# First layer's output product: two of four weight chunks by seven products of sums

## The chip, the cores and the metric

The kernel runs on one core of one Trainium2 chip. The metric is device time of one execution in microseconds (us). The engines named below are PE (matrix products; PEld is its weight load), DVE (elementwise work), ACT (activations, copies, casts), POOL (elementwise work and the issue of some DMAs) and SP (the issue of the other DMAs). Each runs its own instruction queue in order; semaphores join them.

## The reference

Two layers of a block with sparse attention, multi-scale pooling and a gated sum, on 16 meta tokens and 512 tokens (T = 528) with D = 1024. What bears on this change is the last line of a layer, and the norm that begins the next:

```python
def rms_norm(x, g):
    xf = x.astype(jnp.float32)
    y = xf * lax.rsqrt(jnp.mean(xf * xf, axis=-1, keepdims=True) + EPS)
    return (y * g.astype(jnp.float32)).astype(x.dtype)
...
    g_a, g_b = jnp.split(jax.nn.sigmoid(merge), 2, axis=-1)
    return x + jnp.einsum('btd,de->bte', g_a * y_a + g_b * y_b, w_out)
```

The output product multiplies the merged branches M (528 tokens by 1024) with `w_out` (1024 by 1024) and adds it to the residual. All values are float32.

## The kernel before, in words

**Precision by parts.** PE multiplies in a reduced form (fp32r). Each operand is therefore kept as a high part (a cast) and a low part (value minus high part), and a product is three matmuls: high by high, high by low, low by high. The merged branches lie transposed, 8 blocks k of 128 features by 528 tokens, in `hhi` and `hlo`. The high parts are cast by ACT (L1479), the low parts are subtracted by POOL, and for the last block by DVE.

**Weights** come in chunks of 256 output columns (for `w_out`), each loaded by SP as two `raw` tiles from a ring of four, and split into `w` tiles from a ring of eight. A tile's place is free for the next load or split when its last reader is done. There are three ways to split a chunk. In the plain one ACT casts (L206) and DVE subtracts (two `w<-raw,w` of 128x1024). For the chunks in `by_dma` ACT writes the negated cast (L220), a DMA issued by POOL adds the raw values onto it in place (L221), and ACT casts again (L225); DVE does nothing. For the chunks in `mixed`, `mixed_prep` (L257) forms sums of the four blocks of the weight matrix: one by a DMA that adds in place before the rest (`first_sum`, L255), the others by DVE and one more DMA (L284). ACT casts seven operands (L269), and DVE subtracts seven low parts of 128x512.

**Two forms of product.** `dense` (L596) multiplies one block of 128 output columns with one half of the tokens: 8 k blocks by 3 = 24 matmuls into one of three PSUM banks `d`. `group_of_products` (L1044) takes a chunk of 256 columns by two halves of the tokens as a 2x2 block product done with seven products instead of eight (Strassen's scheme as Winograd ordered it): 7 products of 4 k blocks by 3 = 84 matmuls. Its operands on the token side are the four quarters of the left matrix and sums of them. The first layer's gates use it already, with 264 tokens a half (`mix_gates`), and so does the second layer's output product for its last two chunks (`sums_of_merged` and `mix_out`, 256 tokens a half). `product` (L1054) calls weight preparation until the operand that it needs has been issued.

**The first layer's end.** After the gates, two chunks of branch A are multiplied (L1468): for each of 8 blocks j and each half, 12 matmuls, then on DVE `ta` = (`ta` + 1) times the product, plus `zb` (both in `ta`), the cast to `hhi` on ACT and the low part `hlo` on POOL. Then POOL makes the tables of the next layer (`tables`, L481: `gk`, `Cg`, `Sg`). The output product follows: chunks 0 and 1 in `dense` form for both token halves (272 and 256), then chunks 2 and 3 together, the first half of the tokens for all four column blocks, then the second half. After each group DVE adds it to the residual (`res`), ACT squares it (`tq`), POOL adds up the squares (`sqs`). After the first half's last group `stats` (L1517) sums the squares over the features on PE, POOL takes the power, and `norm_half` (L511) turns the result on PE, multiplies on DVE (8 blocks `nf`), casts on ACT and subtracts low parts on DVE and POOL, with the low part of a block three blocks behind its product. This runs beside the second half's products. The next layer starts with `plain_trio` (L579), products of `nf` in plain float32, and goes on with `tok_group`, which needs `hhi` and `hlo`.

**Order.** PE and DVE run in the order in which the code records them: `later(fn, n)` puts work n groups on, `group_done` runs what is due and one item of weight preparation. ACT, POOL and SP are ordered by a scheduler. All recorded calls of PE and DVE carry the line of a helper, L63, so they are told apart by their tiles.

Of the kernel before, what the change touches and what calls it, by code (L numbers as in the profile page):

```python
# [11 lines left out]
OP = mybir.AluOpType  # L12
# [79 lines left out]
def tile_block(ctx: ExitStack, tc: tile.TileContext, x, meta, w_in, pool_w, w_a, w_b, w_out, rows, hgain, c_tab, out):  # L92
# [10 lines left out]
    def f(ap):  # L103
        return ap.bitcast(F32)
# [406 lines left out]
    def norm_half(l, hf, rstd, lag=1, pool=(1, 3, 5, 7), warm_up=False):  # L511
# [11 lines left out]
        nf = [NF[0][k // 4][:, k % 4, a:a + n] for k in range(KT)]  # L523
        for k in range(KT + lag):
            if k < KT:
                t = nf[k]
                dve.scalar_tensor_tensor(t, RES[0][:, k, a:a + n], parT[:, l * 8 + k:l * 8 + k + 1], rb[:, :n],
                                         op0=OP.mult, op1=OP.mult)
                end = act.copy(hhi[:, k, a:a + n], t)
            if k >= lag:  # L530
                j = k - lag
                (gp if j in pool else dve).tensor_sub(hlo[:, j, a:a + n], nf[j], f(hhi[:, j, a:a + n]))
        return end.ins
# [61 lines left out]

    def dense(w, mt_, a, n, rhs=H, kt=KT, late=False):  # L596
        ps = bank("d")
# [5 lines left out]
        for e, (ww, r, k) in enumerate(steps):  # L603
            pe.matmul(ps[:, :n], ww[k][:, c], r[:, k, a:a + n], start=e == 0, stop=e == len(steps) - 1)
            if (e + 1) % (len(steps) // parts) == 0 and e + 1 < len(steps):
                (group_done if (e + 1) * 4 // len(steps) == 2 and parts == 4 else half_done)()
        return ps

# [527 lines left out]

    def sums_of_merged(ta):

        c0, c1 = slice(16, 272), slice(272, 528)
        t1 = one.tile([128, 2, 4, 256], F32R, tag="D", name="osum1")  # L1140
        t4 = []
        t2 = [tmp.tile([128, 4, 128], F32R, tag="P", name="osum2", bufs=PB).rearrange("p (s a) c -> p s (a c)", s=2)
              for _ in range(4)]
        t3 = [tmp.tile([128, 544], F32R, tag="L", name="osum3", bufs=LB)[:, :512].rearrange("p (s c) -> p s c", s=2)
              for _ in range(4)]

# [5 lines left out]

        def sums(k):
            a0, a1, b1 = ta[k][:, c0], ta[k][:, c1], ta[4 + k][:, c1]
# [13 lines left out]
        def last_high(k):  # L1168
            if not t4:
                t4.append(one.tile([128, 2, 4, 256], F32R, tag="C", name="osum4"))  # L1170
            act.copy(t4[0][:, 0, k], ta[4 + k][:, c0])
# [25 lines left out]

    def mix_out(operands):
        base = popped[0] - progress[W["use"]]
        for q in range(2):  # L1200
            def add(eh, t, src):
                j = 4 + 2 * q + eh
                d = RES[0][:, j, 16 + 256 * t:272 + 256 * t]
                dve.scalar_tensor_tensor(d, src, -0.5 if eh else 0.5, d, op0=OP.mult, op1=OP.add)
                later(lambda: turned_out(j, t), 2)

            def total(eh, t, ps, part):
                o = sheet(256, "c")[:, :256]
                dve.tensor_tensor(o, ps[:, :256], part, op=OP.add)
                add(eh, t, o)  # L1210

            group_of_products(q, base, 256, operands, total, add)

# [57 lines left out]
    for l in range(2):  # L1271
# [196 lines left out]
        for c in range(2):  # L1468
            w = chunk()
            if l and c:  # L1470
                first, sums, lows, fourth, last_high, last_low, operands = sums_of_merged(ta)
# [21 lines left out]
        if l == 0:  # L1493
# [4 lines left out]
            dve.memset(mm, 1.0)  # L1498
            def out_group(w, mi, j, halves):
                for hf, a, n, o in halves:  # L1500
                    ps = dense(w, mi, a, n, late="k" if j == hf == 0 else False)
                    d = RES[0][:, j, a:a + n]
                    dve.scalar_tensor_tensor(d, ps[:, :n], 0.5, d, op0=OP.mult, op1=OP.add)
                    if j == 0:
                        act.activation(sq[:, a:a + n], d, AF.Square, scale=D ** -0.5)
                    elif j < KT - 1:
                        t = tmp.tile([128, HB], F32, tag="tt", name="tq", bufs=6)
                        act.activation(t[:, :n], d, AF.Square, scale=D ** -0.5)
                        gp.tensor_tensor(sq[:, a:a + n], sq[:, a:a + n], t[:, :n], op=OP.add)
                    else:  # L1510
# [17 lines left out]

            for c in range(2):
                w = chunk()  # L1530
                for mi in range(2):
                    out_group(w, mi, 2 * c + mi, halves)
            w2 = chunk()
            flush_prep()
            w3 = chunk(ahead=False)
            for hs in (halves[:1], halves[1:]):
                for c, w in ((2, w2), (3, w3)):
                    for mi in range(2):
                        out_group(w, mi, 2 * c + mi, hs)
                    if c == 2 and hs[0][0] == 1:  # L1540
                        w_prep_enqueue()
                if hs[0][0] == 0:
                    later(lambda: stats(0), 1)
                    later(lambda: norm_half(1, 0, mm, LAG2), 2)
            hooks = {0: lambda: stats(1), 1: lambda hf: None if hf else norm_half(1, 1, mm, LAG3)}
        else:
# [34 lines left out]
            later(lambda: [last_low(k) for k in (2, 3)], 4)  # L1581
            mix_out(operands)
            rows(1, 4, w, flush)
# [52 lines left out]
```

## Time and profile before

| | |
|---|---|
| median of 3 runs (lowest to highest) | 734.21 us (733.96 to 734.82) |
| the profiled execution's own time | 735.03 us |
| its span in the trace | 733.2 us |
| mean granted PE clock | 1.00 |
| PE busy, share of the span | 723.7 us, 99% |
| DVE / ACT / POOL busy | 597.2 / 491.4 / 262.3 us |
| output product of the first layer | 328.4 to 377.2 us in the trace |

Rows of a timeline are: start, duration, engine, line, operation, output tile <- input tiles, shapes, how many were merged, and in brackets how long the engine sat idle before and what ended that. The profile models the end of a matmul, so a row's duration there overlaps with the next; rates of PE are taken from one start to another. The same holds for DVE, where one instruction's end overlaps with the start of the next.

### The profile page before, as it was taken

The page shows a single profiled execution, that of the slowest core. Times are in us where ns is not written, and L with a number is a line of the kernel's source. Part 1 is how long each engine was busy: PE and PEld are TensorE (multiplying, and loading weights), DVE is VectorE, ACT ScalarE, POOL GpSimd, SP SyncE. Part 2 cuts the span into 40 slices and gives each one's busy share as a digit, 9 for nine tenths or more (in the row PEclk, how much of TensorE's full clock was granted, in tenths as well). Part 3 has the DMA queues.
Part 4 walks back from the last instruction along what each step waited for, and adds up shares of the span by engine and source line. Part 5 has one row for each costly group of instructions (what it writes and reads, how often), then busy time and mean ns, then how long its engine had stood idle before and what let it go on. Part 6 is the DMA issues. An engine that isn't in the chain of part 4 may idle for free.

```text
span 733.2 us, 15958 instructions
## 1 busy us (share of the span) xinstructions
PE 723.7 (99%) x5853; PEld 697.0 (95%) x5853; DVE 597.2 (81%) x1488; ACT 491.4 (67%) x1125; POOL 262.3 (36%) x345
## 2 busy tenths in 40 slices
PE   9999999999999999999999999999999999999998
PEld 8999998899999999999999989998899899999997
DVE  6877999998998875894358779999989988768774
ACT  6779635676888886543246796367788888775643
POOL 3751174721223311173256411857042231116210
PEclk9999999999999999999999999999999999999999
DMA  8777755974655333633422788667564554438832
GB/s 268 234 180 166 168 138 116 238 149 91 148 113 136 81 92 97 211 124 130 132 89 87 180 185 200 155 162 163 112 160 105 134 116 91 113 108 269 201 90 71
DMA packets 103566, 106.41 MB, mean 145 GB/s; under 512 B 5008, under 2 KB 83632, under 8 KB 103488
## 3 DMA queue, kind: packets, MB, share of 16 engines
q1 hardware_dynamic: 91888, 74.89, 33.5%
q0 software_dynamic: 11520, 30.41, 23.4%
q8 instruction: 46, 0.75, 0.4%
q14 instruction: 32, 0.26, 0.1%
q10 hardware_dynamic: 80, 0.08, 0.0%
HBM read 66.41 MB, written 8.55 MB: 102 GB/s over the span
## 4 chain that ended last, share of the span: by engine, by line
PE 79%; DVE 12%; issue 4%; ACT 2%; DMA 2%; POOL 1%; DVEq 0%; POOLq 0%; ACTq 0%
PE d L63 65%; PE a L63 10%; PE v L63 4%; DVE w L63 3%; DVE t L63 1%; DVE lt L63 1%; DMA w<-raw 1%; DVE sc L63 1%; DVE m L63 1%; ACT lt L832 1%; DVE zb L63 1%; DVE nf L63 1%; DVE c L63 0%; DMA raw<-s 0%; DVE sila L63 0%
## 5 line engine op out<-in xcount | busy, mean ns | idle before, releaser
L63 PE MATMUL d<-hhi,w 128*128 128x256 f32 (+3 forms) x1392 | 279.2, 292 | 1.6 <-DVE c L63 1.6
L63 PEld LDWEIGHTS d<-hhi,w 128*128 128x128 f32 x1392 | 222.3, 188 | 5.2 <-DVE c L63 2.0
L63 PE MATMUL d<-hlo,w 128*128 128x256 f32 (+3 forms) x696 | 189.8, 289 | 0.0
L63 DVE TENSOR_TENSOR w<-raw,w 128x512 fp32r<-128x512 f32 (+1 forms) x156 | 121.8, 787 | 14.5 <-ACT w L269 14.3
L63 PEld LDWEIGHTS d<-hlo,w 128*128 128x128 f32 x696 | 131.3, 189 | 1.4 <-issue 0.2
L63 PE MATMUL d<-hsum,w 128*128 128x264 f32 (+1 forms) x720 | 95.1, 285 | 0.2
L63 PEld LDWEIGHTS d<-hsum,w 128*128 128x128 f32 x720 | 89.7, 188 | 1.2 <-issue 0.3
L63 PE MATMUL d<-w,hhi 128*128 128x256 f32 x576 | 86.1, 287 | 0.6 <-DVE w L63 0.6
L269 ACT CAST w<-raw 128x512 fp32r<-128x512 f32 x132 | 78.5, 623 | 3.0 <-DMA raw<-s 2.3
L63 PEld LDWEIGHTS d<-w,hhi 128*128 128x128 f32 x576 | 74.7, 188 | 5.3 <-issue 2.9
L255 POOL DMA_DIRECT2D raw<-raw x22 | 20.5, 931 | 109.3 <-DMA raw<-in_w_in_dram 16.3
L63 DVE MATCH_REPLACE8 sc<-m,sc 128x400 f32<-128x400 f32 (+2 forms) x100 | 54.4, 547 | 0.0
L63 DVE MAX8 m<-sc 128x8 f32<-128x400 f32 (+2 forms) x100 | 53.4, 557 | 0.9
L221 POOL DMA_DIRECT2D w<-raw x34 | 31.8, 966 | 60.9 <-ACT w L220 44.7
L832 ACT ACTIVATE lt<-lt,mn,NR 128x144 f32<-128x144 f32 (+3 forms) x64 | 42.2, 661 | 13.2 <-DVE mn L63 13.0
L63 PE MATMUL d<-mhi,w 128*128 128x272 f32 (+2 forms) x192 | 46.1, 326 | 1.0 <-ACT sq L681 0.9
L63 PE MATMUL d<-w,hlo 128*128 128x256 f32 x288 | 45.5, 281 | 0.0
L284 POOL DMA_DIRECT2D raw<-s x22 | 19.2, 871 | 65.5 <-DVE s L63 29.0
L847 POOL TENSOR_SCALAR pm<-lt,rs 128x16 f32<-128x16 f32 x48 | 28.0, 612 | 38.8 <-DVE rs L63 28.6
L753 ACT ACTIVATE r<-a,wab 128x272 f32<-128x272 f32 (+2 forms) x80 | 35.5, 487 | 8.7 <-PE a L63 8.2
L1481 POOL TENSOR_TENSOR hlo<-ta,hhi 128x256 fp32r<-128x256 f32 (+1 forms) x28 | 26.6, 961 | 40.9 <-PE d L63 28.7
L690 POOL TENSOR_TENSOR t<-t,t 128x256 f32<-128x256 f32 (+1 forms) x34 | 30.6, 900 | 24.6 <-DVE t L63 24.3
(259 smaller groups left out, 1566.2 us busy)
## 6 DMA issues: line engine op xcount, KB each, us to landing
raw<-in_w_in_dram SPq DMA_DIRECT2D x88, 256.0 KB, 3.3
w<-raw POOLq DMA_DIRECT2D x34, 512.0 KB, 5.8
raw<-in_w_in_dram SPq DMA_DIRECT2D x32, 512.0 KB, 4.3
raw<-in_w_out_dram SPq DMA_DIRECT2D x12, 512.0 KB, 3.6
raw<-raw POOLq DMA_DIRECT2D x22, 256.0 KB, 4.0
raw<-s POOLq DMA_DIRECT2D x22, 256.0 KB, 3.3
kept<-res SPq DMA_DIRECT2D x16, 264.0 KB, 2.8
res<-kept SPq DMA_DIRECT2D x16, 264.0 KB, 5.2
```

The source lines that it names most:

```text
L63: return fn(*a, **k)
L221: gp.dma_start(t, raws[c][s], accum_op=OP.add)
L255: gp.dma_start(raws[c][0][:, 1], raws[c][0][:, 0], accum_op=OP.add)
L269: act.copy(t[:, 0], blk[src[n]])
L284: gp.dma_start(blk["a12"], blk["s2"], accum_op=OP.add)
L690: added[0] = gp.tensor_tensor(t1[:m, :256], t1[:m, :256], t2[:m, :256], op=OP.add).ins
L753: act.activation(r[:, n - 1::-1] if i == 0 else r[:, o:o + e], ps[:, :e], AF.Relu, scale=wab[:, i, h:h + 1])
L832: act.activation(L[hh][:, :n], L[hh][:, :n], AF.Exp, scale=NR[:, i, h:h + 1], bias=mn[:, hh:hh + 1], accum_out=sm[:, hh:hh + 1])
L847: (gp if j < 3 else dve).tensor_scalar(pms[i][:, 2 * j + hh, :], L[hh][:, 0:16], rs[:, hh:hh + 1], None, op0=OP.mult)
L1481: pool_end = gp.tensor_sub(hlo[:, j, a:a + n], d, f(hhi[:, j, a:a + n]))
```

## The change

Only the first layer's output product and what feeds it are touched.

- Chunk 0 of `w_out` is split `by_dma`; chunks 1 and 2 become `mixed`. These are the second and third of four.
- The token sums that the groups need (`sums_of_merged`, now with the halves' start and width as arguments) are formed from `ta`: first differences (`first`) while branch A's second chunk runs, the other sums, high parts and low parts in four steps beside chunk 0, one after each `dense`.
- Chunks 1 and 2 run as two `group_of_products` of 264 tokens a half.
- Chunk 3 alone runs by token halves (272, then 256). `stats` for the first half goes into the middle of the second half's first group, `norm_half` into the middle of its last. With the argument `KT + 1` `norm_half` issues all eight products and casts first, and the low parts after the group.

```diff
+        if l == 0:
+            by_dma.add(len(chunks) - 4)
+            mixed |= {len(chunks) - 3, len(chunks) - 2}
...
-        for k in range(KT + lag):
+        for k in range(KT + lag % (KT + 1)):
...
+        if lag > KT:
+            return lambda: [low(j) for j in range(KT)]
...
-    def sums_of_merged(ta):
+    def sums_of_merged(ta, s0, n2):
-        c0, c1 = slice(16, 272), slice(272, 528)
+        c0, c1 = slice(s0, s0 + n2), slice(s0 + n2, s0 + 2 * n2)
...
+                if l == 0 and c:
+                    if mi == 0:
+                        prep_one()
+                    first(mi)
...
-            for c in range(2):
-                w = chunk()
-                for mi in range(2):
-                    out_group(w, mi, 2 * c + mi, halves)
-            w2 = chunk()
-            flush_prep()
-            w3 = chunk(ahead=False)
-            for hs in (halves[:1], halves[1:]):
-                for c, w in ((2, w2), (3, w3)):
-                    for mi in range(2):
-                        out_group(w, mi, 2 * c + mi, hs)
...
-                if hs[0][0] == 0:
-                    later(lambda: stats(0), 1)
-                    later(lambda: norm_half(1, 0, mm, LAG2), 2)
+            w = chunk()
+            sums(0)
+            sums(1)
+            steps = deque([lambda: [sums(2), sums(3)], lambda: [lows(0), lows(1), fourth_all()],
+                           lambda: [lows(2), lows(3), last_high(0), last_high(1)],
+                           lambda: [last_high(2), last_high(3), last_low(0), last_low(1)]])
...
+            for mi in range(2):
+                out_group(w, mi, mi, halves, None, lambda: steps.popleft()())
+            last_low(2)
+            last_low(3)
+            mix_out(operands, 2, s0, n2, lambda j, t, d: squares(n2 * t, n2, d))
+            w = chunk(ahead=False)
+            for mi in range(2):
+                out_group(w, mi, 6 + mi, halves[:1])
+            w_prep_enqueue()
+            out_group(w, 0, 6, halves[1:], lambda: stats(0))
+            rest = []
+            out_group(w, 1, 7, halves[1:], lambda: rest.append(norm_half(1, 0, mm, KT + 1)), lambda: later(rest[0], 0))
```

What this does to DVE's queue is seen just behind branch A's last low part. In the rows, `osum` tiles hold the token sums' parts, `s` is a sum of weight blocks, `w` a low part of weights. Before, from that low part on (`msq` is a fill of the statistics):

```order
L63 TENSOR_TENSOR hlo<-ta,hhi 128x256
L63 MEMSET msq 128x5
L63 SCALAR_TENSOR_TENSOR res<-d,res 128x272
L63 SCALAR_TENSOR_TENSOR res<-d,res 128x256
L63 TENSOR_TENSOR w<-raw,w 128x1024
L63 SCALAR_TENSOR_TENSOR res<-d,res 128x272
```

Now, the last twelve rows up to the low part of weights that the first group's third product needs (the last row). Ahead of them, behind the same `hlo` row, stand nineteen more instructions of 128x264 and two `res` rows:

```order
L63 TENSOR_TENSOR w<-raw,w 128x512
L63 TENSOR_TENSOR s_5050<-raw 128x512
L63 TENSOR_TENSOR w<-raw,w 128x512
L63 SCALAR_TENSOR_TENSOR res<-d,res 128x272
L63 TENSOR_TENSOR osum_4961<-ta,osum_4961 128x264
L63 TENSOR_TENSOR osum_4964<-ta,osum_4964 128x264
L63 TENSOR_TENSOR osum_4961<-ta,osum_4961 128x264
L63 TENSOR_TENSOR osum_4965<-ta,osum_4965 128x264
L63 TENSOR_TENSOR raw<-s_5050,raw 128x512
L63 SCALAR_TENSOR_TENSOR res<-d,res 128x256
L63 TENSOR_TENSOR osum_4961<-ta,osum_4961 128x264 x4
L63 TENSOR_TENSOR w<-s_5050,w 128x512
```

Between branch A's end and the first group's third product DVE has 27 instructions of 128x264, five of 128x512 and four `res` additions, where it had the four `res` additions and two subtractions of 128x1024.

POOL's queue at the same place, which holds branch A's low parts, the tables and the squares. Before:

```order
L1481 TENSOR_TENSOR hlo<-ta,hhi 128x256
L484 TENSOR_SCALAR gk<-gains 128x64
L494 TENSOR_TENSOR Cg<-consts,gk 128x320
L495 TENSOR_TENSOR Sg<-consts,gk 128x320
L1509 TENSOR_TENSOR sqs<-sqs,tq 128x272
```

Now (the DMAs are the in-place additions of weight blocks; the first belongs to the second group's chunk):

```order
L1502 TENSOR_TENSOR hlo<-ta,hhi 128x272
L258 DMA raw<-raw 128x512
L1502 TENSOR_TENSOR hlo<-ta,hhi 128x256
L1502 TENSOR_TENSOR hlo<-ta,hhi 128x272
L1502 TENSOR_TENSOR hlo<-ta,hhi 128x256
L258 DMA raw<-raw 128x512
L487 TENSOR_SCALAR gk<-gains 128x64
L497 TENSOR_TENSOR Cg<-consts,gk 128x320
L498 TENSOR_TENSOR Sg<-consts,gk 128x320
L287 DMA raw<-s_5050 128x512
L1527 TENSOR_TENSOR sqs<-sqs,tq 128x272
```

Three low parts now stand behind a DMA whose data must have been loaded, and the tables behind a second one.

PE at the layer's border, where the norm's turn (`a<-consts,msq`) goes. Before it stood between two whole groups, two groups from the border's `raw,nf` products; now it stands inside the last group:

```order
L63 MATMUL a<-consts,msq 128x16
L63 MATMUL a<-consts,msq 128x128 x2
L63 MATMUL d<-hhi,w 128x256
L63 MATMUL d<-hlo,w 128x256
L63 MATMUL d<-hhi,w 128x256
L63 MATMUL d<-hlo,w 128x256
L63 MATMUL d<-hhi,w 128x256 x8
L63 MATMUL d<-raw,nf 128x200 x16
```

Twelve matmuls are left between the turn and the first product that reads `nf`.

More of the change, by code (lines that the diff above doesn't have):

```diff
@@ L523, in norm_half, with low @@
         nf = [NF[0][k // 4][:, k % 4, a:a + n] for k in range(KT)]
-        for k in range(KT + lag):
+        def low(j):
+            (gp if j in pool else dve).tensor_sub(hlo[:, j, a:a + n], nf[j], f(hhi[:, j, a:a + n]))
+        for k in range(KT + lag % (KT + 1)):
             if k < KT:
@@ L530, in norm_half @@
             if k >= lag:
-                j = k - lag
-                (gp if j in pool else dve).tensor_sub(hlo[:, j, a:a + n], nf[j], f(hhi[:, j, a:a + n]))
+                low(k - lag)
+        if lag > KT:
+            return lambda: [low(j) for j in range(KT)]
         return end.ins
@@ L1135, in mix_gates, with places @@
                 later(lambda: SIL.update(ready=True), 4)
-    def sums_of_merged(ta):
-        c0, c1 = slice(16, 272), slice(272, 528)
[L1140 to L1145, printed above, removed]
+    def sums_of_merged(ta, s0, n2):
+        c0, c1 = slice(s0, s0 + n2), slice(s0 + n2, s0 + 2 * n2)
+        t1 = one.tile([128, 2, 4, n2], F32R, tag="D", name="osum1")
+        t2, t3, t4 = [], [], []
+        def places():
+            if n2 > 256:
+                both = one.tile([128, 2, 2, 4, n2], F32R, tag="C", name="osum24")
+                t2.extend(both[:, 0, :, k] for k in range(4))
+                t4.append(both[:, 1])
+            else:
+                t2.extend(tmp.tile([128, 4, 128], F32R, tag="P", name="osum2", bufs=PB).rearrange(
+                    "p (s a) c -> p s (a c)", s=2) for _ in range(4))
+            t3.extend(tmp.tile([128, 544], F32R, tag="L", name="osum3", bufs=LB)[:, :2 * n2].rearrange(
+                "p (s c) -> p s c", s=2) for _ in range(4))
+        if n2 <= 256:
+            places()
         def first(k):
@@ L1153, in sums @@
         def sums(k):
+            if not t2:
+                places()
             a0, a1, b1 = ta[k][:, c0], ta[k][:, c1], ta[4 + k][:, c1]
@@ L1169, in last_high @@
             if not t4:
-                t4.append(one.tile([128, 2, 4, 256], F32R, tag="C", name="osum4"))
+                t4.append(one.tile([128, 2, 4, n2], F32R, tag="C", name="osum4"))
             act.copy(t4[0][:, 0, k], ta[4 + k][:, c0])
@@ L1196, in turned_out, with mix_out @@
                           ot[:, :256].rearrange("p (a e) -> p a e", a=2))
-    def mix_out(operands):
+    def mix_out(operands, j0, s0, n2, then):
         base = popped[0] - progress[W["use"]]
@@ L1201, in add @@
             def add(eh, t, src):
[L1202 to L1203 removed]
+                j = j0 + 2 * q + eh
+                d = RES[0][:, j, s0 + n2 * t:s0 + n2 * (t + 1)]
                 dve.scalar_tensor_tensor(d, src, -0.5 if eh else 0.5, d, op0=OP.mult, op1=OP.add)
[L1205 removed]
+                then(j, t, d)
             def total(eh, t, ps, part):
[L1208 to L1209 removed]
+                o = sheet(n2, "c")[:, :n2]
+                dve.tensor_tensor(o, ps[:, :n2], part, op=OP.add)
                 add(eh, t, o)
[L1212 removed]
+            group_of_products(q, base, n2, operands, total, add)
     ss0 = one.tile([128, 5], F32, name="ss0")
@@ L1469, in tile_block @@
             w = chunk()
-            if l and c:
-                first, sums, lows, fourth, last_high, last_low, operands = sums_of_merged(ta)
+            if c:
+                first, sums, lows, fourth, last_high, last_low, operands = sums_of_merged(ta, s0, n2)
             for mi in range(4):
@@ L1498, in tile_block, with squares, out_group @@
             dve.memset(mm, 1.0)
-            def out_group(w, mi, j, halves):
+            def squares(a, n, d):
+                t = tmp.tile([128, HB], F32, tag="tt", name="tq", bufs=6)
+                act.activation(t[:, :n], d, AF.Square, scale=D ** -0.5)
+                gp.tensor_tensor(sq[:, a:a + n], sq[:, a:a + n], t[:, :n], op=OP.add)
+            def out_group(w, mi, j, halves, mid=None, then=None):
                 for hf, a, n, o in halves:
-                    ps = dense(w, mi, a, n, late="k" if j == hf == 0 else False)
+                    ps = dense(w, mi, a, n, late="k" if j == hf == 0 else False, mid=mid)
                     d = RES[0][:, j, a:a + n]
                     dve.scalar_tensor_tensor(d, ps[:, :n], 0.5, d, op0=OP.mult, op1=OP.add)
+                    if then:
+                        then()
                     if j == 0:
@@ L1506, in out_group @@
                     elif j < KT - 1:
-                        t = tmp.tile([128, HB], F32, tag="tt", name="tq", bufs=6)
-                        act.activation(t[:, :n], d, AF.Square, scale=D ** -0.5)
-                        gp.tensor_tensor(sq[:, a:a + n], sq[:, a:a + n], t[:, :n], op=OP.add)
+                        squares(a, n, d)
                     else:
@@ L1581, in tile_block @@
             later(lambda: [last_low(k) for k in (2, 3)], 4)
-            mix_out(operands)
+            mix_out(operands, 4, s0, n2, lambda j, t, d: later(lambda: turned_out(j, t), 2))
             rows(1, 4, w, flush)
```

9 lines of the change are left out of this document (6 added, 3 removed).

## The prediction

> **What bounds the kernel now.** I read the page's busy times first, then the chain of waits, then a table of busy time by stretches, and last the timelines of the engines around the output product. The busy times:
>
> ```profile
> PE 723.7 (99%) x5853; PEld 697.0 (95%) x5853; DVE 597.2 (81%) x1488; ACT 491.4 (67%) x1125; POOL 262.3 (36%) x345
> ```
>
> The chain of waits (start, length, what) through the place that is changed:
>
> ```profile
> 303.26 63.77 PE d L63 x516
> 368.20 2.93 PE d L63 x24
> 371.65 11.08 PE d L63 x80
> ```
>
> PE runs 516 matmuls without a wait from 303.26 to 367.0, and goes on to the border and past it. So time is saved here only by fewer PE matmuls, and whatever makes PE wait is lost in full. The stretches (us, then PE, PEld, DVE, ACT, POOL busy with counts) say how much room the others have. The first is branch A's end, the next two are the output product's chunks 0 and 1:
>
> ```profile
> 317.00:328.40 11.40, 11.40 (x96) 11.40 (x95) 10.72 (x19) 4.96 (x11) 7.78 (x9) 1.00 0.28 93
> 328.40:340.40 12.00, 12.00 (x99) 11.89 (x98) 7.17 (x13) 4.68 (x8) 4.66 (x5) 1.00 0.34 113
> 340.40:352.10 11.70, 11.70 (x98) 11.70 (x97) 4.00 (x6) 4.08 (x7) 3.80 (x4) 1.00 0.42 137
> ```
>
> DVE is nearly full at branch A's end (10.72 of 11.40) and has 4.8 us free in chunk 0. The two traded things are PE matmuls and DVE work, at a place where DVE has little room.
>
> **What PE saves.** The PE timeline gives the first matmul of chunk 0 (328.43), its two groups of the second column block (334.55, 337.55), and the first of chunk 1:
>
> ```profile
> 328.43 0.29 PE L63 MATMUL d<-hhi,w 128*128 128x272 f32 x1
> ...
> 334.55 0.29 PE L63 MATMUL d<-hlo,w 128*128 128x272 f32 x1
> ...
> 337.55 0.28 PE L63 MATMUL d<-hlo,w 128*128 128x256 f32 x1
> ...
> 340.40 0.29 PE L63 MATMUL d<-hlo,w 128*128 128x272 f32 x1
> ```
>
> Twenty-four matmuls of 272 columns take 3.00, twenty-four of 256 take 2.85; a chunk (two of each) takes 11.70. The price of a matmul of 264 columns stands in the first layer's gates, in the chain's pieces there:
>
> ```profile
> 169.26 7.34 PE d L63 x60
> 176.60 0.40 PE a L63 x4
> ```
>
> 7.34 / 60 = 0.1223 each, and 84 x 0.1223 = 10.27 for a group of products. Two chunks save 2 x (11.70 - 10.27) = **2.9 us**. That the change does not do this is ruled out by PE's program: 84 matmuls stand for 96 twice.
>
> **What DVE must do before PE can go on.** Between branch A's last low part and the low part of weights that the group's third product reads, DVE has 27 instructions of 128x264, five of 128x512 and four `res` additions. Durations of such instructions stand in the second layer's output product, where the same sums are made with 256 columns:
>
> ```profile
> 687.10 0.42 DVE L63 TENSOR_TENSOR ta<-ta 128x256 f32<-128x256 f32 x1
> 687.62 0.42 DVE L63 SCALAR_TENSOR_TENSOR ta<-ta 128x256 f32<-128x256 f32 x1
> 687.97 0.42 DVE L63 SCALAR_TENSOR_TENSOR ot<-d,rt 128x256 f32<-128x256 f32 x1
> 688.30 0.41 DVE L63 TENSOR_TENSOR ta<-ta 128x256 f32<-128x256 f32 x1
> 688.63 1.09 DVE L63 TENSOR_TENSOR osum<-ta,osum 128x256 fp32r<-128x256 f32 x3
> ...
> 707.15 1.29 DVE L63 TENSOR_TENSOR w<-raw,w 128x512 fp32r<-128x512 f32 x2
> ```
>
> One more instruction in a merged row adds (1.09 - 0.42) / 2 = 0.335 at 256 columns; with eight more columns I take 0.343: 27 x 0.343 = 9.3. Where one reads what the one before wrote, the next starts 0.52 later instead (687.10 to 687.62); four such pairs add 4 x 0.13 to 0.17, 0.5 together. A `res` addition takes 0.33 (687.97 to 688.30), 0.35 with 272 columns: 1.4. One of 128x512 takes 1.29 less the tail of 0.69, so 0.60: 3.0. Sum **14.2 us**.
>
> When it starts: the stream follows branch A's last low part.
>
> ```profile
> 327.01 1.80 DVE L63 TENSOR_TENSOR w<-raw,w 128x1024 fp32r<-128x1024 f32 x1
> ...
> 331.11 0.41 DVE L63 SCALAR_TENSOR_TENSOR ta<-ta,d 128x256 f32<-128x256 f32 x1
> 331.55 0.66 DVE L63 TENSOR_TENSOR ta<-ta,zb 128x256 f32<-128x256 f32 x1
> 332.69 0.43 DVE L63 TENSOR_TENSOR hlo<-ta,hhi 128x256 fp32r<-128x256 f32 x1 [0.47 <-ACT hhi L1479]
> 333.04 0.43 DVE L63 SCALAR_TENSOR_TENSOR res<-d,res 128x272 f32<-128x272 f32 x1
> ```
>
> Before, it would start at 333.0. The two subtractions of 128x1024 (chunk 0's, the row at 327.01 is the second) leave DVE because chunk 0 is now split by a DMA, but the first differences, some seven instructions or 2.4 us, come in. The earliest start: branch A's last product ends at 328.43, and from its reader to the row after the low part is 333.04 - 331.11 = 1.9, less 0.24 that the 0.66 row lost to something: 330.1. The bounds are 330.1 and 333.0; I take the upper middle, 331.8, since ACT has two casts of weight operands ahead of the last `hhi`.
>
> Then POOL. The rows show what happens when both work on SBUF: a free `ta<-ta,zb`, one that meets a POOL instruction, and that instruction. Behind them stand the tables and a square addition, which POOL now issues beside the stream:
>
> ```profile
> 318.27 0.42 DVE L63 TENSOR_TENSOR ta<-ta,zb 128x256 f32<-128x256 f32 x1
> ...
> 321.86 0.93 DVE L63 TENSOR_TENSOR ta<-ta,zb 128x272 f32<-128x272 f32 x1
> ```
>
> ```profile
> 321.76 0.74 POOL L1481 TENSOR_TENSOR hlo<-ta,hhi 128x256 fp32r<-128x256 f32 x1 [0.80 <-ACT hhi L1479]
> ...
> 329.39 0.54 POOL L484 TENSOR_SCALAR gk<-gains 128x64 f32<-128x64 f32 x1
> 330.02 0.87 POOL L494 TENSOR_TENSOR Cg<-consts,gk 128x320 f32<-128x320 f32 x1
> 330.85 1.08 POOL L495 TENSOR_TENSOR Sg<-consts,gk 128x320 f32<-128x320 f32 x1
> ...
> 341.43 0.74 POOL L1509 TENSOR_TENSOR sqs<-sqs,tq 128x256 f32<-128x256 f32 x1 [1.59 <-ACT tq L1508]
> ```
>
> The DVE instruction ended at 322.79, 0.29 after POOL's: it waited for it. The tables keep POOL for about 2.1 us net of tails, a square addition for 0.7. If none of that meets DVE the stream loses 0, if all does 2.8; some falls on DVE's own waits and on `res` additions that read PSUM, so I take 1.5. The Trainium skill ("SBUF — State Buffer", section "Who interferes with whom") says that DVE and GpSimd share a port pair as an exclusive lock, and that a DVE instruction with two SBUF inputs contends with a GpSimd instruction that reads SBUF. The rows above agree (0.93 against 0.42); taken strictly it puts all 2.8 us into the stream, and the sum would be the second rival's.
>
> So the third product's weights are ready at 331.8 + 14.2 + 1.5 = 347.5. PE would ask for them in the third matmul of the third product: 340.40 + 2 x 1.47 + 0.25 = 343.6. PE waits **3.9 us**, spread over the first three products, with bounds 0.7 (330.1 + 14.2) and 6.4 (333.0 + 14.2 + 2.8).
>
> **The second group.** From there DVE has nine of 128x512 (5.4) and seven of `c` and `res` (2.5) to the same place of the second group, 7.9 us, and PE 5 + 2 products, 10.3. Its first weights stand earlier in that queue and could come one 128x512 late: 0 to 0.7, I take **0.2**.
>
> **The border.** The norm of the first half now ends inside the last group. Its rows before (PE's sums of squares, POOL's power, the turn, DVE's multiplications, the first product that reads them):
>
> ```profile
> 367.84 0.36 PE L63 MATMUL a<-ones,tl 128*128 128x1 f32 x2
> 371.07 0.59 PE L63 MATMUL a<-consts,msq 16*128 16x16 f32 x3
> 377.16 5.58 PE L63 MATMUL d<-raw,nf 128*128 128x200 f32 x32
> ```
>
> ```profile
> 368.53 0.88 POOL L503 TENSOR_TENSOR msq<-msq,mhalf 128x3 f32<-128x3 f32 x1 [5.42 <-DVE msq L63]
> ```
>
> ```profile
> 371.69 1.72 DVE L63 SCALAR_TENSOR_TENSOR nf<-res,parT,a 128x272 f32<-128x272 f32 x4
> ```
>
> From the sums (368.2) over the power (end 369.4) to a possible turn are 1.2 us, and PE has a group of 2.85 between them now. After the turn come twelve matmuls, 12 x 0.119 = 1.4 us; the first `nf` is there 371.69 + 0.43 - 371.07 = 1.05 after the turn starts, then one each 0.43, while PE takes 5.58 / 8 = 0.70 for a block. The cost is nothing as long as DVE has no `res` addition of 0.35 ahead; with one in the way it is up to 0.4. I take 0. The low parts, held back to after the group, are hidden by those 5.58 us.
>
> **POOL's queue.** The DMA that begins the second group's sums stands ahead of three of branch A's low parts, and it needs its `raw` tile loaded. The rows: the cast that frees the ring's place, a load, and the in-place addition's time from issue to landing as a bound for a load in traffic:
>
> ```profile
> 316.27 1.05 ACT L206 CAST w<-raw 128x1024 fp32r<-128x1024 f32 x1 [0.54 <-PE d L63]
> ```
>
> ```profile
> raw<-in_w_in_dram SPq DMA_DIRECT2D x88, 256.0 KB, 3.3
> ```
>
> ```profile
> DMA to landing us min/median/max: 4.5/5.8/9.9
> ```
>
> With chunk 0 split by DMA, the place is free when its addition has landed: 317.5 + 4.5 / 5.8 / 9.9, and 3.3 for the load: 325.3 / 326.6 / 330.7. About 0.9 for issue and two low parts of 0.74 later the last is there at 327.7 / 329.0 / 333.1. PE asks for that block after 13 matmuls of chunk 0, 328.43 + 1.6 = 330.1. So it costs nothing by the median, and 3.0 at worst. Even that 3.0 is not added to the 3.9: DVE goes on with its stream while PE waits, so PE's lateness at the third product stays the larger of the two.
>
> **The sum.** -2.9 + 3.9 + 0.2 = +1.2 us. The profiled execution took 735.0 (span 733.2 and 1.8 around it) and would take 736.2; it lies 0.8 above the median of the runs, 734.21, so on the median I predict **735.4**. What a measurement of this kernel can tell from no change is about 0.2%, 1.5 us; the forecast counts as no change, on the slow side. Its own range, with the start and POOL's share moved by 0.9 together, is 734.5 to 736.3 (1.2 less and more 0.9). All low bounds together give -2.9 + 0.7 = -2.2 (732.0), all high ones -2.9 + 6.4 + 0.7 + 0.4 = +4.6 (738.8).
>
> **Rivals.**
>
> *DVE's stream is mostly hidden* (faster). It starts at 330.1, since DVE keeps up with branch A without the two big subtractions, and POOL's tables run before it or in its gaps (0.5): ready at 344.8, a wait of 1.2, net -1.7: 732.5. For it: 4.8 us of DVE are free in chunk 0 before. Against it: DVE was 10.72 of 11.40 busy just ahead.
>
> *POOL's lock in full* (slower). The tables stand behind a second DMA that waits for a load, so all 2.8 us fall in the stream: 331.8 + 14.2 + 2.8 = 348.8, a wait of 5.2, net -2.9 + 5.2 + 0.2 = +2.5: 736.7. It decides the sign beyond 0.2% from 1.8 us of lost DVE time on. For it: the 0.93 row. Against it: DVE has waits of its own in the stream.
>
> *POOL's queue sets the end*: the low parts come at the worst landing, and DVE is early as in the first rival: -2.9 + 3.0 = +0.1: 734.3. It needs the slowest landing of all.
>
> **Chances.** The forecast 0.43 (of it 0.27 within 0.2%, 0.15 slower, 0.01 faster), the hidden stream 0.25 (0.22 faster, 0.03 same), the lock in full 0.22 (slower), POOL's queue 0.08 (same), something unnamed 0.02 (slower). Faster 0.22, same 0.38, slower 0.40. The range, 732.3 to 738.0, holds the first rival (732.5) at one end, and at the other the lock in full (+2.5) with a start 0.9 later and half of what the second group (+0.15 more) and the border (+0.2) can cost, +3.8; only the corners of the bounds are left out.
>
> **What would show it.** In the changed kernel's profile: 10.27 us of PE for each group apart from waits; PE waiting for DVE's `w<-s` before the third product, near 343 to 348, by about 4 us in all; DVE without gaps from about 332 to 347, with single rows of 0.8 and more beside POOL's tables; no PE wait at the `nf` products. I am wrong if DVE's queue is through before 345, if PE waits longest for POOL's low parts or a DMA, or if the wait at the border is over 0.5.

## The result, and the profile after

The changed kernel takes 744.63 us (median of 4 runs, 743.51 to 745.20), the kernel before 734.52 beside it (733.96 to 735.24): a ratio of 1.0135, 95% interval 1.0118 to 1.0153. It is 10.1 us slower; forecast were 735.4 and a range from 732.3 to 738.0. The profiled execution took 743.51 with a span of 741.7, 8.5 us above before's.

The page's busy times of the changed kernel:

```profile
PE 724.1 (98%) x5829; PEld 695.8 (94%) x5829; DVE 618.0 (83%) x1538; ACT 503.9 (68%) x1159; POOL 265.9 (36%) x351
```

PE has 24 matmuls fewer, as the program says, and is busy no shorter; DVE is busy 21 us longer. Where PE now waits in the first layer's output product, by the view of waits (total, times, longest):

```profile
PE d L63 <- DVE w L63: 4.1, 3, 2.2
PE d L63 <- POOL hlo L1502: 1.4, 1, 1.4
PE d L63 <- ACT p L1080: 0.4, 1, 0.4
```

And each of them in PE's timeline, with the border's first product, which has no wait, last:

```profile
331.99 0.39 PE L63 MATMUL d<-hlo,w 128*128 128x272 f32 x1 [1.42 <-POOL hlo L1502]
...
344.79 0.51 PE L63 MATMUL d<-hhi,w 128*128 128x264 f32 x2 [2.24 <-DVE w L63]
...
348.17 0.51 PE L63 MATMUL d<-osum,w 128*128 128x264 f32 x2 [0.42 <-ACT p L1080]
350.21 5.92 PE L63 MATMUL d<-osum,w 128*128 128x264 f32 x34 [1.53 <-DVE w L63]
...
359.58 0.52 PE L63 MATMUL d<-hhi,w 128*128 128x264 f32 x2 [0.29 <-DVE w L63]
...
383.20 5.07 PE L63 MATMUL d<-raw,nf 128*128 128x200 f32 x29
```

Chunk 0 waits 1.42 for a low part of branch A, the first group 2.24 + 0.42 + 1.53 = 4.19, the second 0.29. The border comes at 383.20 where it came at 377.16. Waits alone do not make the 6.0 us between them. The row at 350.21 shows the next piece: 34 matmuls take 5.92, 0.174 each where 0.122 is the price. The table by stretches shows why; its columns behind the engines' are the granted clock, the DMA share and GB/s:

```profile
350.20:354.70 4.50, 4.49 (x24) 4.49 (x25) 3.23 (x6) 1.22 (x3) 0.86 (x1) 0.62 0.34 117
354.70:359.60 4.90, 4.61 (x39) 4.40 (x38) 3.30 (x6) 2.46 (x5) 1.78 (x2) 1.00 0.31 107
```

Behind the waits the granted clock is 0.62 over 4.5 us, which is 3.4 us at half speed, and then 1.00 again; taken by single microseconds it is 0.50 from 351.2 to 354.2. The chain of waits gives 22 matmuls there 4.48 us, 1.8 more than 22 x 0.122:

```profile
350.21 4.48 PE d L63 x22
```

So the first layer's account reads: groups 2.9 saved; chunk 0's start 0.34 later (328.77 for 328.43), low part 1.42, waits of the groups 4.48, half clock 1.8, and 0.9 that stands in no bracket: +6.0. The 0.9 shows from start to start: each of the five waits costs 0.16 to 0.27 more than its bracket (330.28 to 331.99 are 1.71, of which a matmul is 0.125, so 1.58 for a bracket of 1.42). The other 2.5 us lie behind the border: 356.04 us from the border to the end before, 358.5 now. PE's waits behind the border, first before, then now:

```profile
PE d L63 <- DVE c L63: 1.6, 1, 1.6
PE d L63 <- DVE w L63: 0.6, 1, 0.6
```

```profile
PE d L63 <- DVE w L63: 2.0, 5, 0.9
PE d L63 <- DVE c L63: 1.7, 2, 1.1
PE a L63 <- ACT r L762: 0.9, 1, 0.9
```

These are 4.6 in all for 2.2, which is nearly all of the 2.5.

Now the places that the prediction costed. POOL's queue at branch A's end:

```profile
329.58 0.89 POOL L258 DMA_DIRECT2D raw<-raw  x1 [5.49 <-DMA raw<-in_w_out_dram]
330.20 2.42 POOL L1502 TENSOR_TENSOR hlo<-ta,hhi 128x256 fp32r<-128x256 f32 x3
332.28 1.19 POOL L258 DMA_DIRECT2D raw<-raw  x1
332.91 1.12 POOL L487 TENSOR_SCALAR gk<-gains 128x64 f32<-128x64 f32 x1
334.11 1.16 POOL L497 TENSOR_TENSOR Cg<-consts,gk 128x320 f32<-128x320 f32 x1
...
347.93 1.00 POOL L1527 TENSOR_TENSOR sqs<-sqs,tq 128x256 f32<-128x256 f32 x1 [0.23 <-ACT tq L1526]
```

POOL stands idle for 5.49 us because the second group's DMA needs a `raw` tile that is loaded only at 329.6, near the slow end of the bounds (325.3 to 330.7, by the median 326.6). Three low parts then come in one burst. DVE's queue beside it:

```profile
330.06 2.86 DVE L63 TENSOR_TENSOR ta<-ta,zb 128x256 f32<-128x256 f32 x1
333.39 0.42 DVE L63 TENSOR_TENSOR hlo<-ta,hhi 128x256 fp32r<-128x256 f32 x1 [0.47 <-ACT hhi L1500]
333.73 0.46 DVE L63 TENSOR_TENSOR osum<-ta,osum 128x264 fp32r<-128x264 f32 x1
334.11 1.46 DVE L63 TENSOR_TENSOR ta<-ta 128x264 f32<-128x264 f32 x2
...
347.32 2.23 DVE L63 TENSOR_TENSOR osum<-ta,osum 128x264 fp32r<-128x264 f32 x4
349.48 0.68 DVE L63 TENSOR_TENSOR w<-s,w 128x512 fp32r<-128x512 f32 x1
```

One addition that takes 0.42 alone takes 2.86: it starts with the burst and ends with it. The stream starts at 333.73; its last row starts at 349.48 and, at 0.60 net of its tail, is through at 350.08: 16.3 us. Rows with POOL beside them (1.46 for 0.78 and 0.92 for 0.43 beside the tables, 2.23 for 1.45 beside a square addition) carry 2.0 us of it, and 14.3 are its own.

### The profile page after: what moved, and what is told of

It reads as the page before. It is cut to its first block, busy times and chain, and to the rows that moved or that the text cites. A ratio compares the mean times of both kernels' runs of the same rounds, so it can differ in the third digit from the quotient of the medians.

```text
span 741.7 us, 16029 instructions
## 1 busy us (share of the span) xinstructions
PE 724.1 (98%) x5829; PEld 695.8 (94%) x5829; DVE 618.0 (83%) x1538; ACT 503.9 (68%) x1159; POOL 265.9 (36%) x351
## 4 chain that ended last, share of the span: by engine, by line
PE 82%; DVE 11%; ACT 3%; issue 2%; DMA 1%; POOL 0%; DVEq 0%; SPq 0%; ACTq 0%; POOLq 0%
PE d L63 67%; PE a L63 11%; PE v L63 4%; DVE w L63 3%; DVE ta L63 1%; DVE lt L63 1%; DVE s L63 1%; DVE osum L63 1%; DVE c L63 1%; DMA xt<-in_x_dram 1%; DMA raw<-s 1%; ACT lt L841 1%; ACT w L272 0%; DVE sila L63 0%; DVE sc L63 0%
## 5 line engine op out<-in xcount | busy, mean ns | idle before, releaser
L63 PE MATMUL d<-hhi,w 128*128 128x256 f32 (+3 forms) x1312 | 265.3, 292 | 5.4 <-DVE w L63 3.6
L63 PEld LDWEIGHTS d<-hhi,w 128*128 128x128 f32 x1312 | 209.8, 188 | 9.9 <-DVE w L63 4.9
L63 PE MATMUL d<-hlo,w 128*128 128x256 f32 (+3 forms) x656 | 180.7, 289 | 1.4 <-POOL hlo L1502 1.4
L63 DVE TENSOR_TENSOR w<-raw,w 128x512 fp32r<-128x512 f32 (+1 forms) x162 | 121.9, 760 | 14.4 <-ACT w L272 14.2
L63 PEld LDWEIGHTS d<-hlo,w 128*128 128x128 f32 x656 | 123.7, 189 | 2.9 <-POOL hlo L1502 1.6
L272 ACT CAST w<-raw 128x512 fp32r<-128x512 f32 x144 | 85.9, 623 | 6.1 <-DMA raw<-s 4.8
L258 POOL DMA_DIRECT2D raw<-raw x24 | 22.7, 945 | 122.1 <-DMA raw<-in_w_in_dram 23.1
L224 POOL DMA_DIRECT2D w<-raw x36 | 33.5, 961 | 62.6 <-ACT w L223 43.8
L287 POOL DMA_DIRECT2D raw<-s x24 | 21.2, 882 | 69.9 <-DVE s L63 23.6
L223 ACT ACTIVATE w<-raw 128x1024 fp32r<-128x1024 f32 x36 | 37.5, 1057 | 4.3 <-PE d L63 4.2
```

What stands on the lines that cost most here:

```text
L63: return fn(*a, **k)
L223: act.activation(t, raws[c][s], AF.Copy, scale=-1.0)
L224: gp.dma_start(t, raws[c][s], accum_op=OP.add)
L258: gp.dma_start(raws[c][0][:, 1], raws[c][0][:, 0], accum_op=OP.add)
L272: act.copy(t[:, 0], blk[src[n]])
L287: gp.dma_start(blk["a12"], blk["s2"], accum_op=OP.add)
```

## The experiments

Three causes were to be told apart: POOL's bursts on DVE, the half clock, and whatever costs 2.5 us behind the border; the rival throughout was that DVE's stream is simply too long. Ratios are to the kernel before on the same chip, with 95% intervals; the border is the start of the first product that reads `nf`, and "after it" the rest of the span, both in the profiled execution. In three of the kernels (360.1, 360.0 and the 358.5 with no groups) a half clock of 3.4 us fell behind the border as well. The kernel before has medians from 734.5 to 735.9 on the chips that were used, so medians of different rows compare to about 1 us only.

| kernel | median us | ratio | border | after it |
|---|---|---|---|---|
| before | 734.52 | | 377.16 | 356.0 |
| changed | 744.63 | 1.0135 (1.0118 to 1.0153) | 383.20 | 358.5 |
| second group's DMA late | 742.74 | 1.0101 (1.0075 to 1.0127) | 382.69 | 360.1 |
| PE kept busy | 740.85 | 1.0074 (1.0050 to 1.0099) | 381.23 | 357.5 |
| one group, third chunk | 734.71 | 0.9990 (0.9976 to 1.0004) | 377.06 | 356.3 |
| low parts of sums left out | 738.32 | 1.0038 (1.0024 to 1.0052) | 377.26 | 358.8 |
| DMA and tables late | 739.24 | 1.0056 (1.0035 to 1.0077) | 380.89 | 360.0 |
| tables late | 740.90 | 1.0073 (1.0055 to 1.0090) | 380.21 | 358.6 |
| one group, both late | 733.68 | 0.9981 (0.9967 to 0.9995) | 376.43 | 356.6 |
| no groups | 734.71 | 0.9989 (0.9975 to 1.0003) | 377.27 | 358.5 |
| both late, PE kept busy | 741.39 | 1.0078 (1.0053 to 1.0102) | 378.74 | 361.2 |
| one group, second chunk | 742.62 | 1.0101 (1.0076 to 1.0126) | 384.79 | 356.1 |
| second layer's order as before | 739.24 | 1.0049 (1.0031 to 1.0068) | 384.07 | 354.8 |
| one group, both late, order | 733.10 | 0.9981 (0.9966 to 0.9995) | 375.70 | 355.1 |
| all three causes removed | 736.95 | 1.0021 (1.0007 to 1.0036) | 378.24 | 356.0 |

**The second group's DMA late.** It is tied to stand behind POOL's last low part (`tail`):

```diff
-            first_sum(c + 1)
+            with tc.issue_after(tail[0]) if tail[0] else nullcontext():
+                first_sum(c + 1)
```

> Only the DMA that begins the second group's sums moves: on POOL it now stands behind branch A's last low part instead of ahead of three of them. Theory 1 (that DMA, waiting for its load, holds up the low parts; PE waits 1.4 us for one, and the burst of three holds DVE 2.4 us in one instruction): DVE's stream starts 2.4 us earlier, PE waits 5.6 - 2.4 = 3.2 us, and if the shorter waits keep the clock up another 1.7 us goes: 744.6 - 2.4 = 742.2, or 740.5 with the clock. Rival (the DVE stream is late by its own length, and the low parts would meet it elsewhere): within 0.5 us of 744.6.

Measured: 742.74. The low parts did come early, and the burst that DVE met was another one. DVE's low part and POOL's tables in this kernel:

```profile
330.21 2.61 DVE L63 TENSOR_TENSOR hlo<-ta,hhi 128x272 fp32r<-128x272 f32 x1 [0.49 <-ACT hhi L1501]
```

```profile
330.13 1.57 POOL L498 TENSOR_TENSOR Cg<-consts,gk 128x320 f32<-128x320 f32 x1
330.98 1.53 POOL L499 TENSOR_TENSOR Sg<-consts,gk 128x320 f32<-128x320 f32 x1
```

The third product (counted, here and below, at its third matmul, the first that reads the late low part) starts 0.5 earlier, 349.73 for 350.21, not 2.4. The median is close to the 742.2 of theory 1, but that is luck: the saving behind that number did not happen. What was seen fits the rival's words ("would meet it elsewhere") but not its reason; to split them the tables had to move too.

**Tables late, and both late.** The tables go behind the squares of the last group, into the last chunk:

```diff
-            with tc.issue_after(pool_end.ins):
-                tables(1, True)
...
+            with tc.issue_after(sq_end[0]):
+                tables(1, True)
```

> Only the tables move to the last chunk; the DMA stays ahead of the three low parts. Theory 1: the 2.9 us instruction of DVE stays, but the sums right behind it lose 1.2 us less to the tables: 744.6 - 1.2 = 743.4, or 741.7 if the half clock goes. Rival (the tables cost nothing beside PE's 1.4 us wait for the low part): 744.6.

> On POOL both bursts move: the second group's first DMA goes behind branch A's low parts (as in the run with only that moved) and the tables go to the last chunk, where DVE has room. Theory 1 (a POOL burst holds the DVE instruction that meets it from end to end, wherever the burst stands): the 2.6 us instruction goes, DVE's stream ends 2.2 us earlier than with only the DMA moved, 742.7 - 2.2 = 740.5, and 738.8 if the half clock goes too. Rival (the stream's own length is all that matters): 742.7.

With only the tables moved DVE still meets the low parts' burst, in this kernel with the row

```profile
328.67 3.13 DVE L63 TENSOR_TENSOR hlo<-ta,hhi 128x272 fp32r<-128x272 f32 x1 [0.77 <-ACT hhi L1500]
```

The time is 740.90, 0.8 below the lower of the two values. The third product starts at 348.71, 1.5 earlier than in the changed kernel, where 1.2 was expected; and the half clock stayed but moved, to where PE waits for DVE anyway, so that the matmuls behind it ran at full speed (34 in 4.44):

```profile
343.20:348.00 4.80, 4.71 (x24) 4.50 (x24) 4.80 (x13) 2.64 (x7) 3.89 (x3) 0.64 0.46 113
```

```profile
348.71 4.44 PE L63 MATMUL d<-osum,w 128*128 128x264 f32 x34 [0.72 <-DVE w L63]
```

With both moved the time is 739.24, between the 740.5 and the 738.8 of theory 1. DVE's longest single instruction at branch A's end is 1.0, PE's wait for the low part is gone, and the first group's waits are:

```profile
342.51 0.51 PE L63 MATMUL d<-hhi,w 128*128 128x264 f32 x2 [1.12 <-DVE w L63]
345.88 0.51 PE L63 MATMUL d<-osum,w 128*128 128x264 f32 x2 [0.46 <-ACT p L1081]
347.93 5.93 PE L63 MATMUL d<-osum,w 128*128 128x264 f32 x34 [1.54 <-DVE w L63]
```

The third product starts 1.8 us earlier than with only the DMA moved (349.73 there), 2.2 expected. Theory 1 holds for the bursts. Of the 5.6 us that PE waited in chunk 0 and the first group 3.1 are left. Of these 2.7 are waits for DVE's stream, in which a square addition on POOL still costs 0.8 (a row of 2.25 for 1.45); the rest is the stream's own length. The half clock came in some executions only: the profiled one (742.96, mean granted clock 0.995) had two, and the three with a mean clock of 0.999 to 1.000 took 738.1 to 738.8.

**PE kept busy.** Products of `hhi` with itself into an unread bank, `busy` = 16 ahead of the first group's first product and 14 ahead of its third:

```diff
+        if busy[0]:
+            keep_busy(busy[0])
         product(U, "a11", True)
...
+        if busy[1]:
+            keep_busy(busy[1])
         product(U, "s2", False)
```

> PE gets 16 and 14 products that nobody reads, ahead of the first group's first and third product, where it waits for DVE anyway; all else is the changed kernel. Theory 1 (the granted clock falls to half for 3.4 us because PE idles, which costs half of that): the half clock is gone and 1.7 us with it, 742.9. Rival (PE is paced by DVE and ACT there, so the slow clock costs nothing): 744.6; and if the added products come late themselves, above it.

Measured: 740.85, 2.0 below the 742.9 expected, with 3.0 us less span than the changed kernel. The stretch behind the waits has its full clock, and the same 34 matmuls take 4.41 instead of 5.92:

```profile
349.70:354.20 4.50, 4.44 (x36) 4.45 (x37) 3.18 (x7) 2.62 (x6) 0.89 (x1) 1.00 0.40 123
```

```profile
349.76 4.41 PE L63 MATMUL d<-osum,w 128*128 128x264 f32 x34 [0.56 <-DVE w L63]
```

The border is 1.97 earlier, 1.5 of it in these matmuls and 0.45 in their earlier start. Behind the border 1.0 more is gone (357.5 for 358.5); no edit explains that, and its cause is open. Unread work on PE made the kernel faster: this shows that the slow clock is a cost of its own. The Trainium skill ("TensorE: Matmul & The Clock Gate", section "What's actually happening") has the clock halve after an idle window of about 3.4 us that runs free of the kernel. The length agrees (3.4 us here). The gap does not, and here the measurement decides: no single gap of that length was needed, the longest ahead of the half clock was 2.24 in the changed kernel, and 1.85 with the tables late. Nor did a gap always do it: the kernel with the second chunk as its group (below) had waits of 1.89, 0.45 and 1.54, and a later one of 2.56, and kept 1.00 in its profiled execution. What decides it is open.

**Low parts of the sums left out.** For three of the seven products the high part is read in place of the low, so 12 instructions leave DVE's stream:

```diff
-            "s2": lambda s, k: t2[k][:, s],
+            "s2": lambda s, k: t2[k][:, s if n2 <= 256 else 0],
```

> The twelve low parts of the sums for the products s2, s3 and a22 are left out (their high parts are read in their place), so DVE has 12 x 0.343 = 4.1 us less ahead of the third product's weights. Theory 1 (DVE's stream paces the first group): 4.1 of the 4.2 us of waiting there go, and the half clock with them, 1.7: 738.8. Rival (a DMA, ACT or POOL behind the DVE rows sets the time): 743.5 or more.

Measured: 738.32 (738.8 expected). The border is at 377.26; the one wait left in the first group is

```profile
342.93 0.51 PE L63 MATMUL d<-hhi,w 128*128 128x264 f32 x2 [0.86 <-DVE w L63]
```

beside the 1.3 for POOL's low part. So DVE's stream is what the group waits for, not a DMA behind it, and the clock stays at 1.00.

**One group with cover.** The third chunk alone is a group; chunks 0 and 1 are dense and split by DMA:

```diff
-            by_dma.add(len(chunks) - 4)
-            mixed |= {len(chunks) - 3, len(chunks) - 2}
+            by_dma |= {len(chunks) - 4, len(chunks) - 3}
+            mixed.add(len(chunks) - 2)
...
+            w = chunk()
+            for mi in range(2):
+                out_group(w, mi, 2 + mi, halves)
+            mix_out(operands, 4, s0, n2, lambda j, t, d: squares(n2 * t, n2, d), 1)
```

> Only the third chunk is a group of products; chunks 0 and 1 are split by DMA and multiplied densely, so the sums have two chunks of cover (23 us for a stream of 14) instead of one. Theory 1 (the loss is the missing cover): PE waits for no sum, saving 1.4 us: 734.5 - 1.4 = 733.1, with at most 1.4 lost if POOL's low part is late again. Rival (some 2.5 us of the loss lie in the second layer and come from the new order of the last chunk and the norm): 733.1 + 2.5 = 735.6.

> One group (the third chunk), with both POOL bursts moved as well. Theory 1: the 1.1 us wait for a low part in chunk 0, which was left with one group, goes: 1.1 below the one-group kernel, about 2.0 us below the kernel before on the same chip. Rival (that wait was hidden by a later one): as the one-group kernel, 1.0 below before.

PE waits for no sum in either. The first still waits once, 1.06 for a low part behind the tables' burst, and comes out at 0.9990, which is no clear change; the second waits for nothing up to its border and is faster than before, 0.9981 (0.9967 to 0.9995). The expected 2.0 us below before is met by medians (733.68 against 735.85), 1.4 by the ratio.

**One group without cover.** The second chunk is the group instead, right behind chunk 0:

```diff
-            mixed |= {len(chunks) - 3, len(chunks) - 2}
+            mixed.add(len(chunks) - 3)
+            by_dma.add(len(chunks) - 2)
```

> One group again, but the second chunk instead of the third, so it follows chunk 0 directly and its sums have 12 us of cover instead of 23; the DMA that waited for its load is gone with the second group, the tables stand as in the changed kernel. Theory 1 (cover, not the number of groups, decides): waits of 3.5 to 4.5 us ahead of the group's third product and the half clock, 1.7, less one saving of 1.2: 4 to 5 us above the kernel before. Rival (two groups in a row are the trouble, one is free wherever it stands): as the one-group kernel, 0 to 1 us below the kernel before.

The first group's waits are back:

```profile
343.60 0.51 PE L63 MATMUL d<-hhi,w 128*128 128x264 f32 x2 [1.89 <-DVE w L63]
346.98 0.51 PE L63 MATMUL d<-osum,w 128*128 128x264 f32 x2 [0.45 <-ACT p L1081]
349.03 4.40 PE L63 MATMUL d<-osum,w 128*128 128x264 f32 x34 [1.54 <-DVE w L63]
```

PE waits 3.9 us with one group where it waited 4.2 with two, so it is the cover and not the number. Its 7.4 us above before (1.0101, where 4 to 5 us were expected) are no clean measure of that: the chunk behind it, now split by DMA, came late (2.9 us more of waiting for a DMA), and the half clock that was expected is not in this execution.

**No groups.** All of the change but the groups and their sums: chunk 0 by DMA, last chunk by halves, the norm's new place.

```diff
-            mixed |= {len(chunks) - 3, len(chunks) - 2}
...
-            mix_out(operands, 2, s0, n2, lambda j, t, d: squares(n2 * t, n2, d))
+            for c in (1, 2):
+                w = chunk()
+                for mi in range(2):
+                    out_group(w, mi, 2 * c + mi, halves)
```

> No group of products and no sums: chunks 0 to 2 dense, and of the change only chunk 0 by DMA, the last chunk by halves and the norm's new place. Theory 1 (the 2.4 us that the second layer lost come from the groups' later weight work and their other count of steps): within 0.7 us of the kernel before. Rival (they come from the norm's new place, which pushes its low parts past the border): 2 to 2.5 us above the kernel before.

0.9989: the rival falls. The norm's new place costs nothing that shows, neither at the border (377.27) nor in the time. Its profiled execution waited 1.8 us early in the second layer and had a half clock behind it.

**The second layer's order as before.** The code places the second layer's selection steps by two running numbers that the first layer leaves behind. They were 0.1 and 1.8 at the layers' border before; with two groups the count of steps is another, and they are 0.9 and -0.6 (0.0 and -0.6 with one group). The first is the one that counts: with no groups they are 0.1 and -0.6, and PE's program behind the border is that of the kernel before. They are set back:

```diff
         rate[0], share[0] = R_IDX, FULL
+        if l:
+            credit[0], spare[0] = 0.1, 1.8
```

> The changed kernel with one line more: at the start of the second layer the two numbers from which the code places the second layer's selection steps (credit and spare) are set to what they are there in the kernel before (0.1 and 1.8 instead of 0.9 and -0.6). The recorded order of the second layer behind the border is then that of the kernel before. Theory 1 (the second layer's 2.4 us are this carried-over count, not the hardware): the second layer goes from 358.5 back to 356.0 to 356.7, and the time from 744.6 to 742.2. Rival (the second layer suffers from the late norm and weights): 744.6.

Measured: 739.24, 5.4 us below the changed kernel by medians, 3 more than expected. PE's program behind the border is that of the kernel before, matmul by matmul, and its waits there are now

```profile
PE d L63 <- DVE w L63: 1.2, 1, 1.2
PE d L63 <- DVE c L63: 0.3, 1, 0.3
PE a L63 <- POOL pm L856: 0.2, 1, 0.2
```

and the 0.9 for `r` is gone. What follows the border takes 354.8, 3.7 less than in the changed kernel; the first layer is no faster (its longest wait is 2.98, its border 0.9 later). The profiled execution is the slowest of six (740.63), 2.9 below that of the changed kernel, so 2.5 of the 5.4 stand in no trace. That the order costs time is shown: the work behind the border is the same, and only its order was set back.

**The rest.** Three more kernels combine these edits: both bursts moved with PE kept busy (fewer products than before, since the waits are shorter), one group with both moved and the numbers set back, and two groups with all of it.

```diff
-busy=(16, 14) if j0 == 2 and q == 0 else (0, 0)
+busy=(9, 12) if j0 == 2 and q == 0 else (0, 0)
```

> Two groups with both POOL bursts moved and 9 and 12 unread products of PE in the two waits that are left. Theory 1: no half clock by the wait, so the border comes 1.9 us before that of the run with only the bursts moved (380.9), at 379.0; with the second layer as in the other two-group runs (357.5 to 358.8) the span is 736.5 to 737.8, about 1.5 to 2.5 us above the kernel before. Rival (the half clock of that run was not from PE's waits): border at 380.9.

The border is at 378.74 as expected (379.0) and the half clock is gone, but the rest of the span was 361.2 and the runs lie far apart (738.1 to 743.1). The two numbers are 0.9 and -0.6 at its border as well, and the programs of PE and DVE behind it are those of the changed kernel, which took 358.5 there. Why the same order takes 2.7 longer here is open.

> One group (the third chunk), both POOL bursts moved, and the second layer's order as before. Theory 1: the saving of 1.2 us in the first layer, kept, with the second layer back from 356.6 to 356.0 to 356.3: 1.2 to 1.8 us below the kernel before on the same chip, 2.0 to 2.5 by the run without the reset, which was 2.2 below. Rival (the earlier 2.2 was luck of the chip): no more than 0.7 below.

733.10 against 734.67, 0.9981 (0.9966 to 0.9995): one group with both bursts moved beats both kernels, in two measurements with the same ratio. So the reset, which takes 1.5 us off behind the border in the profiled executions (355.1 for 356.6), adds nothing that the ratio shows. Its group runs from its first product to the last chunk without a wait:

```profile
352.15 0.28 PE L63 MATMUL d<-hlo,w 128*128 128x264 f32 x1
...
362.23 0.29 PE L63 MATMUL d<-hhi,w 128*128 128x272 f32 x1
```

The row at 352.15 is the group's second matmul, so it takes 10.20 (10.27 predicted).

> Two groups with everything that was found to cost: both POOL bursts moved, unread products of PE in the two waits, the second layer's order as before. Theory 1 (POOL's bursts, the half clock and the carried count make up the whole loss beside the plain waits for DVE): border at 378.7 as without the reset, second layer 354.8 to 356.0, span 733.5 to 734.7, so 735.3 to 736.5, within 0.2% above the kernel before. Rival (something else of the two groups is still unnamed): 738 or more.

736.95 against 735.53, 1.0021 (1.0007 to 1.0036), with a span of 734.2 in the profiled execution, inside the 733.5 to 734.7 of theory 1; the median is 0.45 above its range, on a chip where before is 1.0 above its first measure. With the three causes out, two groups are 1.5 us above before: PE still waits 1.1 for DVE's own stream and spends 2.5 more on 21 unread products, against 2.9 saved. The rest of the span is back at 356.0, from 361.2 without the reset.

## Why the prediction was wrong

**The saving** was right: 24 matmuls fewer, and 10.20 us for an undisturbed group where 10.27 was worked out.

**DVE's stream** was right in its length, 14.3 for 14.2, and in its place on the path. **When it starts** was the first term to fail: 333.7 where 331.8 was taken and 333.0 was the upper bound. The bound came from before's rows; the sentence on **POOL's queue** had the late load, and said that its 3.0 "is not added to the 3.9" because DVE goes on with its stream meanwhile. It did not go on. The low parts that had waited came as one burst, and the burst held DVE for 2.4 us. The step had two engines that wait for POOL and followed one of them.

**POOL's lock** cost 2.0 us inside the stream; 1.5 was taken and 2.8 was the full lock of the slower rival. That rival had the direction and the mechanism, and it too looked only at what lies inside the stream, so it gave 736.7.

**PE's wait** was 3.9 in the forecast. By the same count (a chunk 0 of 340.40 - 328.43 = 11.97, so the third product's third matmul due at 328.77 + 11.97 + 3.2 = 343.9; it started at 350.21) PE was 6.3 late. That this lies within the upper bound of 6.4 is luck: the stream started 0.7 later than the bound had it, and the lock cost 0.8 less. Taken with the 6.4 the sum gives +3.7, not +8.5.

**What the sum had no term for** is the larger part of the error, 4.3 of 7.3 us in the span. The half clock behind the waits, 1.8, is nowhere in it: waiting was priced at its own length. And the sum stopped at the border, as if all that follows were moved and not changed; 2.5 us in the profiled execution, and 3.7 by what the reset gave back, came from there, most of it from a recorded order that a carried number had changed.

**The second group** (0.29 for 0.2) and **the border** (no wait at the `nf` products) were right. The faster rival is refuted: nothing of the stream was hidden but what chunk 0 covers.

## What to carry to other kernels

A product that trades matmuls for sums is worth what its cover hides: one group with two chunks ahead of it made PE wait for no sum (0.9990, and 0.9981 with POOL's bursts moved), and with one chunk ahead PE waited 3.9 us, so give the sums their time before counting the saving. Look at what a late transfer holds back on an in-order queue, and then at every engine that the burst behind it holds up. And where code orders later work by running counters, a change in one stage is a change in all stages behind it: compare the recorded order behind the edit, or set the counters back.

## What was not expected of the hardware

- A series of POOL instructions on SBUF held one DVE instruction with two SBUF inputs from its start to the end of the series: 2.86 us beside three of 0.8, 2.61 beside two, 3.13 in a third kernel. It was not let in between them.
- PE's granted clock fell to half for 3.4 us after waits of which the longest was 1.5 to 3.0 us, and the price was 1.8 us where PE was the bound, nothing that shows where it waited for DVE. In the profiled executions it did not fall after single waits of 0.81 to 1.42, and in one kernel neither after 1.89, 0.45 and 1.54 nor after 2.56.
- Filling the waits with 30 unread products on PE gave back 1.5 us of this.
